# Differential attention's score maps: zero-padded query copies against half-height products issued in pairs

## The chip, the cores and the metric
The kernel runs on one core of a Trainium2 chip. It uses five engines with a queue each: TensorE (matrix products, PE in the profile, with its weight loads as PEld), VectorE (DVE), ScalarE (ACT), GpSimd (POOL) and SyncE (SP, which here issues the DMAs of weights). The metric is the device time of one execution in microseconds (us), the median over several runs.

## The reference
The program is the trunk of a diffusion generator: four layers over 256 latent and 256 context tokens of 1024 features, each a token mixer (another one in each layer) and an MLP. The change is in layer 1, differential attention with 8 heads. Cut to that:

```python
def _softmax_probs(q, k, scale):
    s = jnp.einsum("bhqd,bhkd->bhqk", q, k).astype(jnp.float32) * scale
    return jax.nn.softmax(s, axis=-1)

def project(t, positioned):                     # 128 features a head, two halves of 64
    q, k, v = (_heads(a, DIFF_HEADS) for a in jnp.split(t @ w_in, 3, axis=-1))
    if positioned: ...                          # rotates both halves of q and k (latent tokens)
    return q[..., :hd], q[..., hd:], k[..., :hd], k[..., hd:], v

def attend(q1, q2, k1, k2, v):
    p = _softmax_probs(q1, k1, scale) - lam * _softmax_probs(q2, k2, scale)
    o = jnp.einsum("bhqk,bhkd->bhqd", p.astype(v.dtype), v)
    return _rms_norm(o, subln) * (1.0 - lambda_init)
```

Each head has two attention maps, one from the first 64 features of its queries and keys and one from the last 64. Latent queries see the keys of all 512 tokens, context queries those of the 256 context tokens. The mixed map is multiplied with the values, and the result is normalised over the head's 128 features.

## The kernel before, in words
Activations lie with features on partitions and tokens along the columns: 256 latent columns (`S` of them), then 256 context columns (`T2` = 512 in all). Products with weights take operands split into a high and a low part (`mm3`, lines 294 to 296, three products each, the weight's parts made by lines 277 and 278 from 512 KB blocks that SP loads ahead). Everything else in layer 1 is multiplied in full float32, which TensorE runs as two instructions per product.

`mixer1` first makes the values of all heads (`proj_v`), and then runs a loop over 8 heads. Beside the attention of head h the generator `project(h + 1)` makes the next head's queries and keys: per head two blocks (`proj1`, 8 input tiles of three products of 512 columns each), each copied out of PSUM by ScalarE (lines 956 and 963) and rotated by `rope` (a product with a permutation at line 654, then VectorE, lines 655, 656 and 658). `aside(n)` takes its next n steps; in head 7 it takes steps of the output projection instead (`early`).

Queries are kept in `qz`, two sets (for even and odd heads) of two tiles of 128 partitions. Tile e holds the 64 features of map e on their own partitions and zeros on the other 64, written once by four memsets on POOL. So the score product of map e has all 128 partitions of the keys as its other operand, and the zeros take away the half that does not belong. In each head the loop visits the latent queries (two tiles of 128, keys of 512 columns) and then the context queries (two tiles, 256 columns). For one such query tile and each of the two maps:

- line 992: the scores, into a tile of the PSUM pool `sc`, which has two banks in turn;
- `softmax`: VectorE's maximum (line 664) and its factor (665), ScalarE's exponential (666) with the sum read back after it, VectorE's reciprocal (667).

Then VectorE mixes the maps (996 to 998), TensorE transposes the mixed map (1001), ScalarE copies it out of PSUM (1004), and up to three steps of the next head's projections follow in the program. After two query tiles the product with the values is made (1014) and copied (1016). After both streams `finish(h)` normalises the head: a square on ScalarE (971), a sum over partitions on TensorE (646, from `rsqrt_sum`), a scaled copy (647), a logarithm, an exponential and a square on ScalarE, and three VectorE instructions (529, 530, 973).

The order of instructions in each engine's queue is not the order of the program text. A scheduler lays it out when the program is built, going by text order as priority, by its own idea of durations and by when tiles and banks come free; on the chip each engine then takes its queue in that order. `DIFF_ROWS` gives the number of buffers of each ring of tiles: two for `k`, five for `p` (the maps), four for `pt`, four for `x`, two for `f`.

In layer 3, `gdn_chain` has products of 64 partitions: line 1594 takes the two halves of the partitions in turn, each into a bank of its own.

Of the kernel before, what the change touches and what calls it, by code (L numbers as in the profile page):

```python
# [12 lines left out]
F32 = mybir.dt.float32  # L13
# [15 lines left out]
DIFF_ROWS = dict(k=2, p=5, pt=4, x=4, f=2)  # L29
# [18 lines left out]
class Cols:  # L48
    """Column layout of the packed per-feature parameters."""
# [19 lines left out]
def _wa(w, kc=8):  # L69
    """[K, F] -> [F/128, K/(128 kc), 128, kc * 128]: blocks that hold one tile of outputs."""  # L70
    k, f = w.shape
    w = w.reshape(k // (128 * kc), kc, 128, f // 128, 128)
    return np.ascontiguousarray(w.transpose(3, 0, 2, 1, 4)).reshape(f // 128, k // (128 * kc), 128, kc * 128)


def _wb(w):
    """[K, F] -> [F/512, K/256, 128, 2 * 512]: blocks that hold 512 outputs of 256 inputs."""
    k, f = w.shape
    w = w.reshape(k // 256, 2, 128, f // 512, 512)
    return np.ascontiguousarray(w.transpose(3, 0, 2, 1, 4)).reshape(f // 512, k // 256, 128, 1024)  # L80


def _rope(dim):
    """cos and signed sin of the axial positions: [128 features (whole heads), 256 tokens] each."""
# [10 lines left out]
def _layout(x):  # L95
    """Host side: arrays as the kernel reads them (transposed, cut and joined; no arithmetic)."""
# [40 lines left out]
    # rows 0-63 see (forward, backward) in the two passes over a token tile, rows 64-127 the other way round  # L137
# [18 lines left out]
class Trunk:  # L156
    def __init__(self, ctx, tc, ins, out):
        self.ctx, self.tc, self.nc, self.I, self.out = ctx, tc, tc.nc, ins, out
        # what a layer norm is cut into
# [32 lines left out]
    def open_acc(self, pool):  # L192
        """Banks for products in turn from a pool of two and from that for projections beside other work."""
        acc, pj = ("acc", pool("acc", 2, space=PSUM)), ("pj", self.pj)
        turn = cycle((acc, acc, pj, pj))

        def tile():
            n, p = next(turn)
            return p.tile([128, T2], F32, name=n)
        self.acc = tile  # L200

    def proj1(self, block, n=T2, kc=8, x=None, every=2):
        """As proj, for one block and from the pool for projections beside other work; yields after every few input tiles."""
# [20 lines left out]
    def after(self, ins, other):  # L224
        """ins comes after other, of the same engine."""
# [9 lines left out]
    def tables(self):  # L235
        """Loads the tables of exp and ln, both, after the last silu."""
# [5 lines left out]
    def weights(self, *key):  # L242
        """One block of weights, split; the blocks that come after it are loaded and split ahead."""
# [13 lines left out]
    def load(self, name, *at):  # L257
        """Loads one block of weights and splits it: hi + lo, both with at most 12 significant bits; some stay whole."""
# [13 lines left out]
    def halved(self, pool, src, n=""):  # L272
        """Up to 1024 columns from DRAM, split."""
# [7 lines left out]
    def blocks(self):  # L281
        """The blocks of weights in the order of their use."""
# [15 lines left out]
    def proj(self, blocks, n=T2, t0=0, kc=8, x=None, outer=None, spare=False):  # L298
        """Yields PSUM tiles [128 features, n tokens]; blocks: weight blocks, one per output tile.
        outer: output widths of blocks whose products go together, input tile by input tile.  # L300
        spare: the first product goes to another pool."""
# [32 lines left out]
    def ada_prepare(self):  # L334
# [3 lines left out]
        # stationary operands of 32 columns: both conditions, and sums of partitions into one column or the other  # L338
# [8 lines left out]
        # picks the streams' rows from each quarter, or their sums over the quarters  # L347
# [4 lines left out]
    def begin(self, raw, blocks):  # L352
        """The first sub-layer's input, tile by tile as its modulation arrives, and beside it the products with the
        first blocks of weights, which arrive between; returns those products."""
# [57 lines left out]
    def aside(self, n=None):  # L412
        """The next n steps of the modulation that is worked out beside other things."""
        for _ in islice(self.beside, n):
            pass

    def ada(self, i):
        """Modulation of layer i: mods[:, 8 * kind + tile, stream]; yields 8 times for each kind (begin makes the first two of
        layer 0).  The products of layer 0 are TensorE's, those of the others, which come beside an MLP, VectorE's."""
# [37 lines left out]
    def coef(self, i, sub, r):  # L457
        """u = n * A + B and the gate for layer i, sub-layer sub, stream r; n is -2 times the normalised stream, without gain."""
# [28 lines left out]
    def ln_add(self, d, a, b):  # L487
        """Takes columns a to b of tile d of z, complete (the first two tiles come with all their columns).
        Sums are about c, the mean of the features of the first two tiles; it is taken from the others beforehand."""
# [19 lines left out]
    def ln_finish(self, a, b):  # L509
        """Mean (of what is left of z) and -2 / deviation of columns a to b."""  # L510
# [11 lines left out]
    def rsqrt(self, out, x):  # L522
        """out = -2 (x + eps) ** -0.5: the tables' value and one Newton step; x is overwritten."""
# [15 lines left out]
    def coefs(self, i, sub, t=T2):  # L539
        """All that turns the normalised parts into the input of a sub-layer, and its gates."""  # L540
# [3 lines left out]
    def enter(self, sub, r):  # L544
        """u (split) and the residual of a sub-layer from stream r, normalised."""
# [21 lines left out]
    def last_tiles(self, blocks, x, kc, sub):  # L567
        """The last four output tiles before a layer norm, part by part: what follows it begins with one
        part while the other is still under way.  sub: what follows, or None at the end."""
# [22 lines left out]
    def last_part(self, sub):  # L592
        """What is left of a layer norm, to be made once the next sub-layer has begun."""
# [6 lines left out]
    def mlp(self, i, t, following=None):  # L600
        """following: makes the coefs of the sub-layer after it, which is entered."""
# [40 lines left out]
    def rsqrt_sum(self, out, s, n, t):  # L642
        """out = -2 (sum over partitions of s / n + eps) ** -0.5, on all partitions; s is overwritten."""
# [6 lines left out]
    def rope(self, x, swapped, tab, out):  # L650
        """x: [128, >= 256] in SBUF; swapped: scratch; out: list of (destination, partitions)."""
# [8 lines left out]
    def softmax(self, p, ps, n, scale):  # L660
        """p = exp(scale * ps - max); returns 1 / sum per partition."""
# [19 lines left out]
    def early(self, name, n=7):  # L681
        """The products of the first n input tiles with the first two blocks of an output projection."""
# [31 lines left out]
    # the order of the projections of the gated linear attention, after the first four  # L714
# [16 lines left out]
    # the order of the other projections of the gated delta rule, after the first keys  # L731
# [15 lines left out]
    def mixer0(self, i):  # L747
        nc, I = self.nc, self.I
        with ExitStack() as ctx:
# [9 lines left out]
            def gather(raw, blocks):  # L759
                """Copies of products and the sum of their squares."""  # L760
# [47 lines left out]
    def mla_heads(self, pool, vp, tab, cq, ck, kr):  # L808
# [7 lines left out]
        def project(quad):  # L816
            """Values of 4 heads, queries and keys of 2 pairs."""
# [32 lines left out]
        for pair in range(8):  # L850
# [6 lines left out]
            for e, (q, k) in enumerate(qk):  # L857
                hp = slice(64 * e, 64 * e + 64)
                pts = []
                for qt in range(4):  # L860
# [14 lines left out]
                    # pt[j][:, kt % 2, query]  # L875
# [19 lines left out]
    def proj_v(self, blocks, dst):  # L895
        """dst[:, token tile, :512] = u^T W, tokens on partitions; blocks: 4 weight blocks of 256 inputs."""
# [18 lines left out]
    def mixer1(self, i):  # L915
        nc, I = self.nc, self.I
        lam0 = 0.8 - 0.6 * math.exp(-0.3 * i)
        with ExitStack() as ctx:
# [16 lines left out]
            qz = [[big.tile([128, T2], F32, name=f"qz{a}{b}") for b in range(2)] for a in range(2)]  # L935
            for a in range(2):
                nc.gpsimd.memset(qz[a][0][64:128, :], 0.0)
                nc.gpsimd.memset(qz[a][1][0:64, :], 0.0)
# [9 lines left out]
            self.sc = pool("sc", 2, space=PSUM)  # L948
# [4 lines left out]
            def project(h):  # L953
                qp = yield from self.proj1(("diff_qk", h, 0))
                x, w, q = row("x"), row("x"), qz[h % 2]
                nc.scalar.copy(x, qp)
                self.rope(x, w, tab, [(q[e][halves[e]], halves[e]) for e in range(2)])
                for e in range(2):
                    nc.vector.tensor_copy(q[e][halves[e], S:], x[halves[e], S:])
# [19 lines left out]
            for h in range(8):  # L979
# [3 lines left out]
                for lat in (True, False):  # L983
# [3 lines left out]
                    for qt in range(2):  # L987
                        qa = (0 if lat else S) + 128 * qt
                        es = []
                        for e in range(2):  # L990
                            sc = self.sc.tile([128, T2], F32, name="sc")
                            nc.tensor.matmul(sc[:, :n], lhsT=q[e][:, qa:qa + 128], rhs=k[:, k0:T2], start=True, stop=True)
                            p = row("p")
                            es.append((p, self.softmax(p, sc, n, scale)))
                        (p, r1), (p2, r2) = es
# [21 lines left out]
                finish(h)  # L1017
            self.split(self.uh[:, 7], self.ul[:, 7], o[:, 7])

# [1 line left out]
    def mixer2(self, i):  # L1021
        nc, I = self.nc, self.I
        with ExitStack() as ctx:
# [84 lines left out]
            def decays(h, e):  # L1108
                """Of one direction: exp of the running log decays, of their negatives and of those up to the chunk's end."""
# [19 lines left out]
                # over a chunk: columns of e1  # L1129
# [738 lines left out]
```

## Time and profile before

| | |
|---|---|
| runs | 2791.73, 2790.97, 2787.93 us |
| median | 2790.97 us |
| profiled execution | span 2789.6 us, first to last instruction; no other time of it is given |
| TensorE busy | 2691.3 us (96%), 15728 products |
| VectorE busy | 2025.3 us (73%) |
| ScalarE busy | 1255.1 us (45%) |
| POOL busy | 47.9 us |
| DMA | 353.26 MB, mean 127 GB/s |

The profile is one execution on the chip. A group row reads: line, engine, operation, output<-inputs, shapes as partitions x columns (for TensorE rows*columns of the array that are used, then the moving operand), count, then busy time in us and mean ns of one, then idle time ahead of them and what ended it. Ends of products are modelled, and products overlap in the pipeline, so the distance from start to start tells more than a duration. A row of a timeline is its start in us, its length, engine, line, operation, names and count, where consecutive instructions of one kind are merged. A row of stretches has the stretch, its length, and for each engine its busy time with the number of instructions in brackets (PE, PEld, DVE, ACT, POOL), then the granted TensorE clock as a share of full speed (2.4 GHz), the DMA share and GB/s.

### The profile page before, as it was taken

What the parts mean: (1) busy time and instruction counts of PE and PEld (TensorE: products, weight loads), DVE (VectorE), ACT (ScalarE), POOL (GpSimd) and SP (SyncE); (2) the same over time, 40 slices, a digit from 0 to 9 for tenths busy, and PEclk for the clock granted to TensorE, in tenths of its full rate; (3) what the DMA queues carried; (4) which work ended last, traced back from release to release, by engine and by line L of the source; (5) the groups of instructions that cost most, each with busy time, mean ns of one, the idle gap of its engine ahead of it and who ended that gap; (6) DMA issues with size and microseconds to landing.
All of it is one profiled execution on the core that took longest, in us unless ns stands there. A gap on an engine that the chain in (4) does not pass through costs nothing. (4 is left out here: it accounts for less than half of the span.)

```text
span 2789.6 us, 41018 instructions
## 1 busy us (share of the span) xinstructions
PE 2691.3 (96%) x15728; PEld 2166.6 (78%) x15728; DVE 2025.3 (73%) x3908; ACT 1255.1 (45%) x2413; POOL 47.9 (2%) x75
## 2 busy tenths in 40 slices
PE   7999999999999989999999999999999998998998
PEld 5666787788876687888888887887887876657997
DVE  3666798784757799875754489876689897668666
ACT  3544453333545663332454455322354555444544
POOL 0000000000000000000000000000000111000000
PEclk9999999999999999999999999999999898999999
DMA  6533237564121126654311125664322445313453
GB/s 232 174 97 104 78 106 218 180 191 134 59 69 50 34 79 218 197 175 147 93 63 56 58 76 178 199 189 159 117 82 81 158 153 151 107 29 121 159 182 113
DMA packets 125536, 353.26 MB, mean 127 GB/s; under 512 B 37499, under 2 KB 41339, under 8 KB 124828
## 3 DMA queue, kind: packets, MB, share of 16 engines
q1 hardware_dynamic: 121804, 337.00, 38.3%
q0 software_dynamic: 3536, 13.63, 1.3%
q8 instruction: 124, 2.03, 0.3%
q14 instruction: 72, 0.59, 0.1%
HBM read 335.91 MB, written 14.68 MB: 126 GB/s over the span
## 5 line engine op out<-in xcount | busy, mean ns | idle before, releaser
L277 ACT CAST whi<-raw 128x1024 fp32r<-128x1024 f32 (+2 forms) x403 | 410.4, 1023 | 694.0 <-PE acc L295 259.9
L278 DVE TENSOR_TENSOR wlo<-raw,whi 128x1024 fp32r<-128x1024 f32 (+2 forms) x403 | 478.0, 1189 | 199.7 <-ACT whi L277 193.9
L294 PE MATMUL pj<-ul,whi 128*128 128x512 f32 (+1 forms) x1072 | 398.6, 372 | 1.1 <-DVE z L565 1.0
L296 PE MATMUL pj<-uh,wlo 128*128 128x512 f32 (+1 forms) x1072 | 386.9, 361 | 0.6 <-DVE wlo L278 0.6
L295 PE MATMUL pj<-uh,whi 128*128 128x512 f32 (+1 forms) x1072 | 386.2, 360 | 0.0
L438 DVE SCALAR_TENSOR_TENSOR acc<-raw,s,acc 128x1024 f32<-128x1024 f32 x252 | 317.2, 1280 | 31.8 <-DMA raw<-in_ada 28.7
L294 PE MATMUL acc<-ul,whi 128*128 128x512 f32 (+3 forms) x888 | 311.7, 351 | 15.9 <-DVE ul L554 11.0
L295 PE MATMUL acc<-uh,whi 128*128 128x512 f32 (+3 forms) x888 | 308.7, 348 | 0.0
L296 PE MATMUL acc<-uh,wlo 128*128 128x512 f32 (+3 forms) x888 | 308.5, 347 | 0.0
L294 PEld LDWEIGHTS pj<-ul,whi 128*128 128x128 f32 x1072 | 203.0, 189 | 37.4 <-issue 6.3
L296 PEld LDWEIGHTS pj<-uh,wlo 128*128 128x128 f32 x1072 | 203.0, 189 | 32.6 <-issue 4.6
L295 PEld LDWEIGHTS pj<-uh,whi 128*128 128x128 f32 x1072 | 203.2, 190 | 30.1 <-issue 5.8
L294 PE MATMUL pj<-hl,whi 128*128 128x512 f32 (+1 forms) x560 | 198.3, 354 | 0.7 <-DVE hl L621 0.3
L294 PEld LDWEIGHTS acc<-ul,whi 128*128 128x128 f32 (+2 forms) x888 | 167.2, 188 | 40.6 <-DVE ul L554 12.9
L295 PE MATMUL acc<-hh,whi 128*128 128x512 f32 (+1 forms) x560 | 197.5, 353 | 0.0
L294 PE MATMUL acc<-hl,whi 128*128 128x512 f32 (+1 forms) x560 | 196.8, 351 | 0.0
L295 PE MATMUL pj<-hh,whi 128*128 128x512 f32 (+1 forms) x560 | 196.7, 351 | 0.0
L296 PE MATMUL acc<-hh,wlo 128*128 128x512 f32 (+1 forms) x560 | 196.5, 351 | 0.0
L296 PE MATMUL pj<-hh,wlo 128*128 128x512 f32 (+1 forms) x560 | 196.2, 350 | 0.0
L296 PEld LDWEIGHTS acc<-uh,wlo 128*128 128x128 f32 (+2 forms) x888 | 167.1, 188 | 22.1 <-issue 1.2
L295 PEld LDWEIGHTS acc<-uh,whi 128*128 128x128 f32 (+2 forms) x888 | 167.3, 188 | 20.8 <-issue 1.0
L620 ACT CAST hh<-t 128x512 fp32r<-128x512 f32 (+1 forms) x128 | 72.2, 567 | 123.6 <-DVE t L619 123.2
(463 smaller groups left out, 5001.0 us busy)
## 6 DMA issues: line engine op xcount, KB each, us to landing
raw<-in_w SPq DMA_DIRECT2D x256, 512.0 KB, 4.2
raw<-in_ada SPq DMA_DIRECT2D x192, 512.0 KB, 4.7
raw<-in_diff_qk SPq DMA_DIRECT2D x16, 512.0 KB, 3.5
raw<-in_gdn_v SPq DMA_DIRECT2D x16, 512.0 KB, 4.0
raw<-in_gdn_z SPq DMA_DIRECT2D x16, 512.0 KB, 4.5
raw<-in_gdn_out SPq DMA_DIRECT2D x16, 512.0 KB, 3.9
raw<-in_mla_in SPq DMA_DIRECT2D x9, 512.0 KB, 7.5
raw<-in_mla_qb SPq DMA_DIRECT2D x12, 384.0 KB, 3.6
```

Source lines behind the costliest of these rows:

```text
L277: nc.scalar.copy(hi[:, :width], raw[:, :width])
L278: nc.vector.tensor_sub(lo[:, :width], raw[:, :width], hi[:, :width].bitcast(F32))
L294: mm(ps, lhsT=ah, rhs=bl, start=start, stop=False)
L295: mm(ps, lhsT=ah, rhs=bh, start=False, stop=False)
L296: mm(ps, lhsT=al, rhs=bh, start=False, stop=stop)
L438: nc.vector.scalar_tensor_tensor(acc[r], w, self.s[:, k, r:r + 1], acc[r], op0=ALU.mult, op1=ALU.add)
L620: nc.scalar.copy(hh[:, f, :t], r[:, :t])
```

## The change
The four `qz` tiles and their memsets go. The rotated query of a head is one tile of all 128 partitions, from the ring `k`, which has four buffers now, shared by queries and keys. The score product of map e takes partitions 0 to 63 or 64 to 127 of both queries and keys. The score pool has one buffer of two banks in place of two of one bank; both products of a query tile are issued one after the other in the text, each into a bank of this tile, and both softmaxes follow. `finish(h - 1)` stands behind the first score products of head h, not at the end of head h - 1; the last head's stands behind the loop. All else in the diff is comments and docstrings that become empty lines.

```diff
-DIFF_ROWS = dict(k=2, p=5, pt=4, x=4, f=2)
+DIFF_ROWS = dict(k=4, p=5, pt=4, x=4, f=2)
...
-            qz = [[big.tile([128, T2], F32, name=f"qz{a}{b}") for b in range(2)] for a in range(2)]
-            for a in range(2):
-                nc.gpsimd.memset(qz[a][0][64:128, :], 0.0)
-                nc.gpsimd.memset(qz[a][1][0:64, :], 0.0)
...
-            self.sc = pool("sc", 2, space=PSUM)
+            self.sc = pool("sc", 1, space=PSUM)
...
-                x, w, q = row("x"), row("x"), qz[h % 2]
+                x, w, q = row("x"), row("x"), row("k")
                 nc.scalar.copy(x, qp)
-                self.rope(x, w, tab, [(q[e][halves[e]], halves[e]) for e in range(2)])
-                for e in range(2):
-                    nc.vector.tensor_copy(q[e][halves[e], S:], x[halves[e], S:])
+                self.rope(x, w, tab, [(q, slice(0, 128))])
+                nc.vector.tensor_copy(q[:, S:], x[:, S:])
...
-                        es = []
-                        for e in range(2):
-                            sc = self.sc.tile([128, T2], F32, name="sc")
-                            nc.tensor.matmul(sc[:, :n], lhsT=q[e][:, qa:qa + 128], rhs=k[:, k0:T2], start=True, stop=True)
-                            p = row("p")
-                            es.append((p, self.softmax(p, sc, n, scale)))
-                        (p, r1), (p2, r2) = es
+
+                        both = self.sc.tile([128, 2, T2], F32, name="sc")
+                        scs = [both[:, e] for e in range(2)]
+                        for sc, hp in zip(scs, halves):
+                            nc.tensor.matmul(sc[:, :n], lhsT=q[hp, qa:qa + 128], rhs=k[hp, k0:T2], start=True, stop=True)
+                        if h and lat and qt == 0:
+                            finish(h - 1)
+                        (p, r1), (p2, r2) = [(p, self.softmax(p, sc, n, scale)) for sc in scs for p in [row("p")]]
...
-                finish(h)
+            finish(7)
             self.split(self.uh[:, 7], self.ul[:, 7], o[:, 7])
```

## Rows read from the trace of the kernel before

**Rows 1.** Stretches: head 3, head 7, and the sum over all eight heads.
```profile
862.90:885.40 22.50, 22.46 (x95) 15.79 (x94) 17.01 (x51) 13.22 (x33) 0.00 (x0) 1.00 0.15 47
...
954.80:975.00 20.20, 18.82 (x74) 11.93 (x74) 12.26 (x40) 12.25 (x33) 0.00 (x0) 1.00 0.00 1
sum 180.20, PE 177.86 PEld 124.10 DVE 135.50 ACT 105.19 POOL 0.00; mean PE 22.23 PEld 15.51 DVE 16.94 ACT 13.15 POOL 0.00
```

**Rows 2.** Groups by line and shape, 794 to 976 us.
```profile
L992 PE MATMUL sc<-k,qz 128*128 128x512 f32 x64 | 33.0, 602 | 0.0
...
L992 PEld LDWEIGHTS sc<-k,qz 128*128 128x128 f32 x128 | 22.4, 189 | 11.3 <-issue 4.3 <-ACT p L666 3.1 <-DVE k L658 0.2
L666 ACT ACTIVATE p<-sc,sm 128x512 f32<-128x512 f32 x32 | 22.1, 691 | 6.7 <-DVE sm L665 6.6
L664 DVE TENSOR_REDUCE sm<-sc 128x1 f32<-128x512 f32 x32 | 22.1, 689 | 18.8 <-PE sc L992 18.8
L992 PE MATMUL sc<-k,qz 128*128 128x256 f32 x64 | 17.9, 382 | 0.0
...
L666 ACT ACTIVATE p<-sc,sm 128x256 f32<-128x256 f32 x32 | 15.3, 478 | 12.2 <-DVE sm L665 11.3 <-DVE sm L667 0.4
...
L666 ACT ACTIVATION_READ_ACCUMULATOR p<-sc,sm 128x1 f32 x64 | 12.9, 201 | 0.0
L664 DVE TENSOR_REDUCE sm<-sc 128x1 f32<-128x256 f32 x32 | 12.8, 418 | 10.4 <-PE sc L992 10.1
...
L665 DVE TENSOR_SCALAR sm<-sm 128x1 f32<-128x1 f32 x64 | 9.3, 147 | 0.4
...
L658 DVE TENSOR_TENSOR qz<-x 64x256 f32<-64x256 f32 x14 | 5.8, 415 | 0.1
```

**Rows 3.** Waits, 795 to 975 us: us in total, times, longest.
```profile
PEld ax L1001 <- DVE p L998: 7.7, 15, 1.6
...
PEld st L646 <- ACT f L971: 4.8, 8, 0.6
...
PEld sc L992 <- ACT p L666: 3.1, 11, 0.6
```

**Rows 4.** Timeline of TensorE, first latent query tiles of head 1.
```profile
820.10 1.02 PE L992 MATMUL sc<-k,qz 128*128 128x512 f32 x2
...
821.19 0.40 PE L295 MATMUL pj<-uh,whi 128*128 128x512 f32 x1
821.42 0.40 PE L296 MATMUL pj<-uh,wlo 128*128 128x512 f32 x1
821.66 1.08 PE L992 MATMUL sc<-k,qz 128*128 128x512 f32 x2
...
822.81 0.39 PE L295 MATMUL pj<-uh,whi 128*128 128x512 f32 x1
```

**Rows 5.** Timeline of TensorE, second context query tile of head 1.
```profile
834.25 1.03 PE L992 MATMUL sc<-k,qz 128*128 128x256 f32 x4
...
835.34 0.39 PE L295 MATMUL pj<-uh,whi 128*128 128x512 f32 x1
```

**Rows 6.** Timeline of TensorE: half-height products in layer 3, full-height ones in layer 1.
```profile
2392.56 1.13 PE L1594 MATMUL st<-t,kt 64*128 64x256 f32 x8
2393.62 0.60 PE L1607 MATMUL ax<-t,at 128*128 128x128 f32 x3
...
967.60 1.89 PE L1014 MATMUL st<-pt,v 128*128 128x256 f32 x8
969.33 0.38 PE L1001 MATMUL ax<-ident,p 128*128 128x128 f32 x2
```

**Rows 7.** Timeline of TensorE in head 7: latent scores, and the last sum of squares.
```profile
954.86 1.02 PE L992 MATMUL sc<-k,qz 128*128 128x512 f32 x2
...
958.19 1.10 PE L992 MATMUL sc<-k,qz 128*128 128x512 f32 x2
...
973.51 1.12 PE L646 MATMUL st<-f,ones 128*128 128x512 f32 x2
```

## The prediction
> **What bounds the kernel now.** I read the stretches by head first. In a head of the middle of layer 1's loop, 22.5 us long, TensorE is busy 22.46 us at full granted clock, VectorE 17.0 (76%), ScalarE 13.2; over all eight heads TensorE has 177.9 of 180.2 us [rows 1]. So TensorE sets the end of heads 0 to 6. Only the last head is open: 1.4 us of its stretch are without TensorE [rows 1].
>
> Then the groups by line, for the scores of line 992: 64 instructions of 512 columns and 64 of 256 [rows 2]. The shape `128*128` is the point: all rows of the array are used, and half of them multiply the zeros of `qz`. One product in full float32 is two instructions, so there are 32 maps of each width.
>
> Then the waits. TensorE's weight loads wait 7.7 us for the mixed map ahead of the transposes, 4.8 for the square ahead of the sum of squares, 3.1 for an exponential that frees a score bank [rows 3]: little beside 180 us.
>
> **The scores.** Durations of TensorE's rows overlap, so I take distances between starts. One latent map: from 820.10 to the second weight product at 821.19 is 1.09 us for two score instructions and one weight product; weight products follow each other at 0.23 (821.19 to 821.42), so the map holds TensorE 0.86 us. The next map, alone among weight products, runs from 821.66 to 822.81: 1.15 - 0.23 = 0.92, or 0.06 for its own change of operand kind [rows 4]. A latent query tile costs 0.86 + 0.92 = 1.78. Two context maps stand together: 834.25 to 835.34 less one weight product is 0.86 [rows 5].
>
> Do two maps on the two halves of the partitions run at once? Layer 3 has the same form: line 1594 multiplies 64 rows at a time, from either half in turn, into two banks. Eight such instructions of 256 columns take 1.06 us until the next line starts; eight of full height (line 1014) take 1.73 [rows 6], 0.216 each. Four in succession would be 0.86, so the halves overlap fully and 0.20 goes into beginning and end. That group began after a wait; for leaving a running stream of weight products I add the 0.06 of rows 4. A joint pair then costs 0.86 + 0.26 = 1.12 for a latent tile and 0.43 + 0.26 = 0.69 for a context tile: 0.66 and 0.17 saved. Heads 0 to 6 have 14 of each: 14 x 0.83 = 11.6 us. Bounds: with nothing lost at the borders 14 x (0.92 + 0.43) = 18.9; with no overlap and the border still paid, a loss of 14 x (0.20 + 0.26) = 6.4. I stay by line 1594, the nearest row.
>
> Rows 6 hold a group that entered an empty array. On that the Trainium skill ("TensorEngine Tiling (Array Packing)", Tiling Modes) speaks against the change: tiles run in parallel, but a change of the tiling mode drains the engine. If nothing of a pair could be loaded before that drain, a weight load of 189 ns [rows 2] would show at each of 28 pairs, 5.3 us, and the sum below would be -3.6 in place of -8.9. No row shows a switch by rows out of weight products.
>
> **The single score tile.** Both banks are now one buffer. The next pair waits until the second exponential has read; before, each map waited for its own bank's. That is later by one exponential and its sum, 0.69 + 0.20 [rows 2]. Behind the waiting pair TensorE has everything in its queue: weight products, transposes, values. The cover is that a head has 48 weight products (11 us), which the order, fixed when the program is built, lays between. Now 3.1 us in 11 places are lost in this way [rows 3]; I add half of that, 1.5 (0, if the products between suffice, to 28 x 0.89 = 25).
>
> **The transposes.** They need the mixed map, for which VectorE takes the maximum of the first map, then of the second (689 ns each, a 147 ns factor behind each). That the second map is there 0.86 us sooner helps nothing while VectorE works on the first. So TensorE comes up to 0.66 sooner to a transpose whose input comes no sooner. If all 15 waits of now [rows 3] grew so, about half of them latent, it would be 8 x 0.66 + 7 x 0.17 = 6.5 us; if weight products fill it, 0. I take a third, 2.0.
>
> **finish moved.** The norm of head h - 1 (a sum on TensorE, five ScalarE and three VectorE instructions) comes after the next head's first scores are issued. The 0.6 us per head in which the load for the sum waits for the square [rows 3] lies partly beside a running score instruction (0.43); the rest, 0.2, goes seven times: -1.3. What is late next is that head's first exponential, queued on ScalarE behind the square, as it is now.
>
> **Edits at nothing.** The rotation writes one tile, not two halves: 14 additions of 415 ns [rows 2] become 7, and the copies of line 959 halve too; 2.9 us of VectorE and more, hidden while TensorE bounds, and a help where (d) below comes about. The four memsets on POOL lie ahead of the loop, beside the value projections; uncovered they would be a gain. No DMA is added or moved, and SP's queue stays as it is.
>
> **Head 7.** It is nearer to a chain: 18.65 us from its first score at 954.86 to the last sum at 973.51 [rows 7], with 42 weight products as filler, and the single tile forbids scores ahead. From the first latent tile to the second there are 3.33 us (954.86 to 958.19); the new cycle is a pair 1.12, two maxima and factors 1.68, an exponential and its sum 0.89, or 3.7. I set +0.5 (-3 if TensorE still bounds, as in the other heads, to +4 with 1 us lost per tile).
>
> **Sum.** -11.6 + 1.5 + 2.0 - 1.3 + 0.5 = -8.9 us against the profiled span of 2789.6, so 2780.7. The median of the runs shown is 1.4 above that span: 2782.
>
> **The rivals.**
> (a) All of it comes through: enough weight products lie between, no wait is added, head 7 gains its share: 16 x 0.83 + 1.3 = 14.6, so 2776. For it: 48 products of 0.23 against four cycles that need 1.7 to 2.6 us of cover each. Against it: an order that was fixed ahead. Chance 0.18.
> (b) The order swallows it: where TensorE gets ahead it waits for VectorE, 6.5 instead of 2.0, and 3.1 instead of 1.5 for the tile: -2.8, so 2788. The waits of rows 3 are many and short, as where an input is awaited just in time. Chance 0.18.
> (c) The maps don't overlap here, something standing between them in the queue. Only borders are left, 0 to +6.4: 2794. Line 1594 speaks against it. Chance 0.07.
> (d) Slower: the single tile makes VectorE and ScalarE one chain. A latent cycle is 3.7, a context one 0.69 + 2 x 0.42 + 2 x 0.15 + 0.48 + 0.20 = 2.5, together 12.4 per head; VectorE's other work is 17.0 - 0.4 - 5.6 (its part of the cycles) = 11.0. If none of that fits into the gaps of the cycles a head takes 23.4, and with some 0.2 for each of four hand-overs to VectorE 24.2, against 22.5. It decides from where VectorE hides less than 1.7 us per head; at half a microsecond hidden it is +1.2 per head, +8 in all: 2799. Against it: each pair is itself such a gap, 3.6 us per head. Chance 0.11.
>
> **How the numbers follow.** My forecast has 0.46, by itself 2779 to 2786. The range, 2774 to 2796, takes in (a), (b) and most of (c) and leaves out (d). A measurement of this kernel tells about 0.2% (5.6 us) from no change. Faster by more (under 2785.4): of mine 0.40, of (a) 0.17, of (b) 0.03, so 0.60. Slower by more (over 2796.6): 0.09 of (d) and 0.02 of (c), so 0.11. The rest, 0.29, is the same.
>
> **What would show it.** In the trace after: score instructions in 64 rows, the four of a tile holding TensorE 1.0 to 1.2 us (latent) and 0.6 to 0.75 (context); heads of 21.3 to 21.7 us in place of 22.5; the scores' wait for exponentials at 4 to 5 us, the transposes' for the mixed map near 10, the sum's for the square near 0; VectorE near 80% of a head. It is wrong if the four starts of a latent tile lie 0.43 apart in single file (c), if heads grow with TensorE idle ahead of scores (d), or if the loop shrinks and a later layer gives it back.

## The result, and the profile after

The changed kernel is slower: 2831.44 us against 2791.35 for the kernel before in the same comparison, a ratio of 1.0148 (95% interval 1.0134 to 1.0161), four runs each. 2782 was predicted, with a range to 2796. The profiled spans are 2827.9 and 2789.6.

Nearly all of it arises in layer 1's loop. From the first score product to the second instruction of the last sum of squares there were 179.2 us (794.89 to 974.05) and are now 215.8 (796.67 to 1012.48), so 36.6 of the 38.3 us. What lies behind the loop takes 1815.5 us in both traces. The other 1.8 us lie ahead of the loop, which starts between 790.5 and 796.7 us in the fourteen profiles of this case; they tell nothing.

Stretches of the changed kernel (columns as in [rows 1]): heads 2 to 7, each from its first score to the next head's, the last to its sum of squares. Heads 0 and 1 have 24.73 and 25.42 us at full clock.
```profile
846.82:872.72 25.90, 22.48 (x94) 15.24 (x93) 17.16 (x49) 13.56 (x34) 0.00 (x0) 0.93 0.13 40
872.72:897.64 24.92, 21.40 (x96) 14.21 (x95) 17.15 (x49) 13.46 (x34) 0.00 (x0) 1.00 0.15 43
897.64:923.67 26.03, 22.83 (x95) 15.27 (x95) 17.16 (x49) 13.48 (x34) 0.00 (x0) 0.93 0.12 41
923.67:952.96 29.29, 26.16 (x104) 17.89 (x103) 21.00 (x55) 17.42 (x41) 0.00 (x0) 0.88 0.11 36
952.96:978.18 25.22, 20.10 (x79) 12.74 (x78) 15.25 (x47) 11.19 (x31) 0.00 (x0) 0.86 0.06 21
978.18:1012.48 34.30, 25.63 (x62) 14.46 (x62) 13.14 (x40) 12.41 (x32) 0.00 (x0) 0.65 0.00 1
```
Head 3 stands against the first row of [rows 1]: 24.92 us for 22.50, with TensorE busy 21.40 for 22.46. So 3.5 us of that head are now without TensorE, where there was next to nothing (0.04), and VectorE and ScalarE have what they had (17.15 and 13.46 us). No engine got more work in this head; they wait for one another. The column behind POOL is the granted clock: it was 1.00 throughout the loop before, and falls below that in heads 2, 4, 5, 6 and 7.

Waits of the changed kernel, 796 to 1014 us (us in total, times, longest):
```profile
ACT p L666 <- DVE sm L665: 48.1, 39, 4.5
DVE sm L667 <- ACT p L666: 35.0, 43, 1.5
...
PEld sc L988 <- ACT p L666: 26.6, 19, 4.8
...
PEld ax L997 <- DVE p L994: 10.7, 14, 1.9
...
PEld st L646 <- ACT f L966: 4.5, 6, 0.8
```
The third row answers to the scores' wait of [rows 3]: 26.6 us, and up to 4.8 at a time, where 3.1 and at most 0.6 were lost. The two rows above it go together: ScalarE's exponential waits for VectorE's factor (48.1 us; 17.9 before), and VectorE's reciprocal for ScalarE's exponential (35.0; 1.5 before). Before, over 795 to 975 us:
```profile
ACT p L666 <- DVE sm L665: 17.9, 18, 4.3
...
DVE sm L667 <- ACT p L666: 1.5, 4, 0.5
```
That is what a chain between two engines looks like: each of them waits for the other, neither is full.

One latent query tile of the changed kernel, head 2 (timeline of all engines, some rows; the brackets have idle time and what ended it):
```profile
853.26 1.13 PE L988 MATMUL sc<-k 64*128 64x512 f32 x4
...
855.47 0.68 DVE L664 TENSOR_REDUCE sm<-sc 128x1 f32<-128x512 f32 x1
...
856.92 0.69 ACT L666 ACTIVATE p<-sc,sm 128x512 f32<-128x512 f32 x1 [1.23 <-DVE sm L665]
...
857.73 0.16 DVE L667 RECIPROCAL sm<-sm 128x1 f32<-128x1 f32 x1 [0.85 <-ACT p L666]
857.81 0.67 DVE L664 TENSOR_REDUCE sm<-sc 128x1 f32<-128x512 f32 x1
...
858.79 0.15 DVE L665 TENSOR_SCALAR sm<-sm 128x1 f32<-128x1 f32 x1
...
858.97 0.69 ACT L666 ACTIVATE p<-sc,sm 128x512 f32<-128x512 f32 x1 [0.34 <-DVE sm L665]
...
859.80 0.70 PE L988 MATMUL sc<-k 64*128 64x256 f32 x4 [2.73 <-ACT p L666]
```
Both maps' scores are there at 854.39. The second map's maximum begins at 857.81, 3.4 us later, right behind the first map's exponential, and the next tile's scores only behind the second map's. The two maps' softmaxes do not overlap at all: from pair to pair 2.21 us to the first maximum (the scores, and VectorE's work on what went before), 1.45 to the first exponential, 0.81 for it, 1.24 for reciprocal, second maximum and factor, 0.83 for the second exponential. That is 6.54 us for one of four tiles of a head.

Granted clock in head 7 of the changed kernel (stretches of 4 us):
```profile
976.00:980.00 4.00, 3.98 (x16) 2.11 (x16) 1.82 (x4) 1.37 (x3) 0.00 (x0) 1.00 0.00 0
980.00:984.00 4.00, 0.37 (x1) 0.00 (x0) 1.78 (x7) 3.53 (x7) 0.00 (x0) 1.00 0.00 0
984.00:988.00 4.00, 3.42 (x7) 1.55 (x8) 3.19 (x7) 1.11 (x4) 0.00 (x0) 0.51 0.02 4
988.00:992.00 4.00, 4.00 (x8) 1.98 (x7) 1.29 (x4) 1.20 (x4) 0.00 (x0) 0.50 0.01 2
```
The score product that this stretch of idling ends with:
```profile
984.32 2.07 PE L988 MATMUL sc<-k 64*128 64x512 f32 x2 [3.95 <-ACT p L666]
```
TensorE does nearly nothing for 4 us, because its next score product waits 3.95 us for an exponential; then it has work again, but at 0.50 of the clock, the lower level of 1.2 GHz. There the two score instructions of a map that stands alone take 2.07 us; at full clock they take 1.12 (848.33, in the kernel with half height alone below).

### The profile page after: what moved, and what is told of

The parts are those of the page before. It is cut to its first block, busy times and chain, and to the rows that moved or that the text cites. A ratio compares the mean times of both kernels' runs of the same rounds, so it can differ in the third digit from the quotient of the medians.

```text
span 2827.9 us, 41019 instructions
## 1 busy us (share of the span) xinstructions
PE 2701.5 (96%) x15728; PEld 2167.5 (77%) x15728; DVE 2023.5 (72%) x3892; ACT 1257.1 (44%) x2413; POOL 46.2 (2%) x71
## 5 line engine op out<-in xcount | busy, mean ns | idle before, releaser
L294 PE MATMUL pj<-ul,whi 128*128 128x512 f32 (+1 forms) x1072 | 391.9, 366 | 0.7 <-DVE sm L665 0.5
```

Source lines behind the costliest of these rows:

```text
L294: mm(ps, lhsT=ah, rhs=bl, start=start, stop=False)
```

## The experiments

Theory A: the one tile of two banks is the cause. It has three variants. A1: VectorE's second maximum waits for ScalarE's first exponential because both read the same tile. A2: the next pair waits until both maps have been read. A3: the reciprocal stands ahead of the second maximum in VectorE's queue. The rivals: B, the moved `finish`; C, the half-height products and the changes between them and full height. None of the kernels leaves out part of the computation.

**Two tiles of one bank** (after, changed):
```diff
-            self.sc = pool("sc", 1, space=PSUM)
+            self.sc = pool("sc", 2, space=PSUM)
-                        both = self.sc.tile([128, 2, T2], F32, name="sc")
-                        scs = [both[:, e] for e in range(2)]
+                        scs = [self.sc.tile([128, T2], F32, name="sc") for e in range(2)]
```


> The changed kernel, but with two one-bank score tiles (a pool of two) in place of one two-bank tile; the half-height products are still issued one behind the other, finish still moved. Theory A (readers of one PSUM tile are kept in text order across engines, so VectorE's maximum of map 1 waits for ScalarE's exponential of map 0, and the four query tiles of a head become chains of 6.3 us): the wait is gone, heads fall from 25.5 to 21.5-22.5 us, no stretch of the loop at half clock, 2778 to 2790 us. Theory B (finish at its new place holds up the first softmax): still 2815 to 2831. Theory C (half-height products leave TensorE so little activity that its clock is halved): half-clock stretches stay in the loop, 2810 to 2831.


Measured: 2793.83 against 2787.96, ratio 1.0021 (1.0009 to 1.0032). The same two banks, taken one by one, give back most of the loss (5.9 us above before, where the change has 40.1): the loop has 183.2 us, at full clock throughout. The time is still 4 us above the range that theory A gave; the expected gain is missing, and the second latent tile of a head shows a reason, in seven of the eight heads.
```profile
842.98 1.12 PE L987 MATMUL sc<-k 64*128 64x512 f32 x2 [0.48 <-ACT p L666]
...
844.70 1.12 PE L987 MATMUL sc<-k 64*128 64x512 f32 x2
```
Its two maps stand apart (x2 each, 1.72 us from one to the other, weight products between), and the first waits for its bank. A map that is alone saves nothing by its half height (the kernel with half height alone, below, has its price).

**The text of the softmaxes interleaved, still one tile** (after, changed):
```diff
-  (p, r1), (p2, r2) = [(p, self.softmax(p, sc, n, scale)) for sc in scs for p in [row("p")]]
...
+  for m, sc in zip(ms, scs):
+      nc.vector.reduce_max(m[:, 0:1], sc[:, :n], axis=AX.X)
+      nc.vector.tensor_scalar_mul(m[:, 1:2], m[:, 0:1], -scale)
+  for m, sc, x in zip(ms, scs, (p, p2)):
+      nc.scalar.activation(x[:, :n], sc[:, :n], AF.Exp, scale=scale, bias=m[:, 1:2], accum_out=m[:, 2:3])
+  for m in ms:
+      nc.vector.reciprocal(m[:, 3:4], m[:, 2:3])
...
```


> The changed kernel with its single two-bank tile, but the text takes both maxima, both factors, both exponentials, both reciprocals in this order. Theory A (order of readers): VectorE's second maximum no longer waits; what is left of the single tile is that the next pair waits for both exponentials, a cycle of 1.12 + 1.68 + 0.69 + 0.89 = 4.4 us for a latent tile in place of 6.4; heads 22 to 23 us, 2783 to 2800. Rival A2 (the joint release of both banks is what costs, not the order of readers): heads stay above 24.5 us, 2815 to 2831.


Measured: 2802.83 against 2787.96, 1.0055 (1.0034 to 1.0075), loop 193.9 us. With the same tile, banks and release, text order alone takes off nearly two thirds of the loss (0.93 of 1.48 points), though the time lies 3 us above the range of theory A. Of the 0.55 that are left, the kernel with two tiles still has 0.21; the rest is the joint release, A2, and that the first exponential now waits for the second maximum, which no run separates. Waits of this kernel, 794 to 990 us:
```profile
PEld sc L988 <- ACT p L997: 13.0, 14, 3.0
...
ACT p L997 <- DVE sm L994: 10.3, 4, 2.8
```
The last row is that wait, in four places: line 994 is the maximum, line 997 the exponential.

**`finish` back at the head's end** (after, changed):
```diff
-                        if h and lat and qt == 0:
-                            finish(h - 1)
...
-            finish(7)
+                finish(h)
```


> The changed kernel with finish(h) back at the end of each head. Theory A: the chain of readers is untouched, 2824 to 2838. Theory B (the moved finish is the cause): 2778 to 2795.


Measured: 2835.82, 1.0169 (1.0142 to 1.0196), loop 226.8 us. B falls: put back, it is no faster. The intervals of this and of the change overlap a little, so that the move helps is likely, not shown.

**Half height alone** (after, with two one-bank tiles, each map's product and softmax in the text order of before, `finish` at the head's end):
```diff
...
+  for e in range(2):
+      sc = self.sc.tile([128, T2], F32, name="sc")
+      nc.tensor.matmul(sc[:, :n], lhsT=q[halves[e], qa:qa + 128], rhs=k[halves[e], k0:T2], start=True, stop=True)
+      p = row("p")
+      es.append((p, self.softmax(p, sc, n, scale)))
...
```


> The kernel before, with one query tile and half-height score products, but its own order: scores and softmax of map 0, then of map 1, in two one-bank tiles, finish at the end of a head. Theory A: no chain; where the two maps are apart in TensorE's queue they don't overlap, where they stand together they do: 2783 to 2793, clock full in the loop. Theory C (half-height products lower the clock): stretches at half clock in the loop, 2800 to 2830.


Measured: 2805.61, 1.0061 (1.0038 to 1.0084). Slower than theory A allowed, and inside the range of C. Three heads of this kernel as a stretch, and one latent map of it:
```profile
844.27:918.56 74.29, 73.50 (x284) 44.54 (x283) 50.60 (x147) 41.38 (x100) 0.00 (x0) 1.00 0.14 43
```
```profile
848.01 0.39 PE L296 MATMUL pj<-uh,wlo 128*128 128x512 f32 x1
848.33 1.12 PE L988 MATMUL sc<-k 64*128 64x512 f32 x2
849.38 0.50 PE L294 MATMUL pj<-ul,whi 128*128 128x512 f32 x1
849.71 0.40 PE L295 MATMUL pj<-uh,whi 128*128 128x512 f32 x1
```
Here TensorE is full (73.50 of 74.29) at full clock, which it has over the whole loop, and yet a head has 24.76 us. So half height does not bring the clock down, as C had it, but it has a price of its own: from the product before to the second one behind there are 1.70 us, less two products of 0.23 is 1.24 for a lone map. By the same reckoning the full-height map of [rows 4] has 0.93 (821.42 to 822.81, 1.39 less 0.46). Such a head has four lone latent maps at 1.24 and two lone context maps at 0.82 (853.03 to 854.31 in this kernel, less 0.46); against 1.78 and 0.86 for a tile before that makes 2.2 us more, an estimate, and the head is longer by 2.1.

**The single tile alone** (the kernel before, changed; queries stay full height with zeros):
```diff
-            self.sc = pool("sc", 2, space=PSUM)
+            self.sc = pool("sc", 1, space=PSUM)
...
+                        both = self.sc.tile([128, 2, T2], F32, name="sc")
+                        scs = [both[:, e] for e in range(2)]
```
with both products first and both softmaxes behind. That order by itself is in the kernel with two tiles and, at full height, in a twin with four banks further down (+0.08%) too, and costs nothing like this.


> The kernel before with one edit: the single two-bank score tile, both score products issued one behind the other and both softmaxes after them. Queries stay in the zeroed copies, products at full height, finish at the end of a head. Theory A (the shared tile chains VectorE and ScalarE): the harm comes without any half-height product; heads of 25 to 28 us, half clock in the last heads, 2825 to 2850 us. Theory C (half-height products are the cause): 2786 to 2796.


Measured: 2848.51 against 2788.15, 1.0216 (1.0199 to 1.0233), loop 238.1 us. This part alone costs more than the whole change. Waits, 796 to 1035 us:
```profile
ACT p L666 <- DVE sm L665: 41.5, 37, 2.9
...
DVE sm L667 <- ACT p L666: 36.6, 49, 1.4
PEld sc L992 <- ACT p L666: 34.5, 23, 5.0
```
The same three rows as in the changed kernel, without any half-height product. A holds, and what else the change does helps beside it: 2.16% less 1.48% is 0.7%. Some of that lies in the queries, their lower products and smaller rotation: the changed kernel with `finish` put back, which differs from this one in them and their buffers alone, has 1.69% (1.0142 to 1.0196).

**Reciprocals last, still one tile** (after, changed: per map maximum, factor and exponential):
```diff
-  (p, r1), (p2, r2) = [(p, self.softmax(p, sc, n, scale)) for sc in scs for p in [row("p")]]
+  for m, sc, x in zip(ms, scs, (p, p2)):
+      nc.vector.reduce_max(...); nc.vector.tensor_scalar_mul(...); nc.scalar.activation(...)
+  for m in ms:
+      nc.vector.reciprocal(m[:, 3:4], m[:, 2:3])
```


> The changed kernel with its single tile; the text is changed so that both reciprocals stand after both exponentials. Theory A1 (the tile: the second maximum is given a wait for the first exponential because both read one tile): the wait moves from the reciprocal to the second maximum and nothing is won, 2822 to 2840 us. Rival A3 (the reciprocal of map 0 stands in VectorE's queue ahead of the second maximum and blocks it): the second maximum goes ahead, heads near 23.5 as where all maxima came first, 2795 to 2810.


Measured: 2821.16, 1.0114 (1.0099 to 1.0129), loop 211.6 us. A3 is at most the smaller part: the reciprocal has gone from ahead of the second maximum, which is worth 0.34 points, far from the range of A3; for the rest the wait has only moved to the maximum itself (line 994 now; 794 to 1008 us):
```profile
DVE sm L994 <- ACT p L996: 22.9, 23, 1.5
PEld sc L988 <- ACT p L996: 19.8, 18, 4.1
```
The built instruction streams say it outright. VectorE's, for one tile, with what each instruction waits for (instructions of other work between them left out):
```
changed kernel                            reciprocals last                      two tiles
L664 TENSOR_REDUCE sm<-sc  [PE]           L994 TENSOR_REDUCE sm<-sc [PE]          L664 TENSOR_REDUCE sm<-sc [PE]
L665 TENSOR_SCALAR         [DVE]          L995 TENSOR_SCALAR        [DVE]         L665 TENSOR_SCALAR        [DVE]
L667 RECIPROCAL            [Activation]   ...                                     L664 TENSOR_REDUCE sm<-sc [PE]
L664 TENSOR_REDUCE sm<-sc  (no wait)      L994 TENSOR_REDUCE sm<-sc [Activation]  L665 TENSOR_SCALAR        [DVE]
```
With one tile the second maximum waits for ScalarE, in the middle stream by itself, on the left through the reciprocal just ahead of it; with two tiles it waits for TensorE alone. It is so in all 32 query tiles of the loop. In these kernels two engines that only read one PSUM tile, each map in a bank of its own, are thus kept in the order of the text. A1 is shown by this, by the two tiles and by the interleaved text (1.14% to 0.55% with the reciprocals last in both); why the build orders two readers I did not find out.

**Four banks: the second query tile of each stream takes its banks from `st`** (two tiles, changed):
```diff
-  scs = [self.sc.tile([128, T2], F32, name="sc") for e in range(2)]
+  pool_, name_ = (self.st, "st") if qt else (self.sc, "sc")
+  scs = [pool_.tile([128, T2], F32, name=name_) for e in range(2)]
```


> The changed kernel with four one-bank score tiles: the first query tile of a pair of tiles takes two from the score pool, the second takes two from the pool of the value products and sums. All products are still issued in pairs, no two maps share a tile, and a pair need not wait for the one before. Theory A with borders as the trace of the kernel after has them (a pair costs 1.25 us latent, 0.82 context, against 1.78 and 0.86): 16 x (0.53 + 0.04) = 9 us less in the loop, some 1 us from finish: 2776 to 2784 where before is 2790; no half clock in the loop. If what is left of the slowness is half-height products as such: 2792 to 2800.

Its twin has the same banks and order, with the zeroed queries of before at full height (shown against the half-height one; it keeps `qz` and its memsets):
```diff
-  nc.tensor.matmul(sc[:, :n], lhsT=q[hp, qa:qa + 128], rhs=k[hp, k0:T2], start=True, stop=True)
+  nc.tensor.matmul(sc[:, :n], lhsT=q[e][:, qa:qa + 128], rhs=k[:, k0:T2], start=True, stop=True)
```


> As the kernel with four score banks, but with zeroed query copies and products of full height (as before): issued together, and unable to overlap. If the overlap is what gains: 2787 to 2793, some 8 us above the half-height one. If the gain is from the banks or the moved finish: equal to it.

Measured: 2791.92, 1.0013 (1.0003 to 1.0024); the twin 2791.39, 1.0008 (0.9999 to 1.0017). No gain, and no difference between the two heights (heads of 22.74 and 22.76 us on average). The second latent pair was split again, since its second bank is held by `finish`'s sum: its weight load waits for the scaled copy of that sum (line 647), 1.0 us in each of four heads. So I moved `finish`, each time with the full-height twin.

**Four banks, `finish` behind the second latent pair:**
```diff
-                        if h and lat and qt == 0:
+                        if h and lat and qt == 1:
```


> As the kernel with four score banks, but finish(h - 1) stands behind the scores of the second latent tile, so that its sum no longer holds one of the two banks which that tile needs: both latent pairs of a head stand one behind the other in TensorE's queue, all 64 rows high. Theory A with borders: both pairs should take about 2.1 us and what follows, against 3.6 at full height, and a head 21.2 to 21.8 us where before has 22.7: 2778 to 2784 where before is 2790. Rival (TensorE no longer bounds a head, VectorE's and ScalarE's chain does, and overlap is won in vain): the products overlap, heads stay at 22.5 or more, 2788 to 2794.

> The same order and banks with zeroed query copies and products of full height. If the overlap of halves is what gains: 2788 to 2794, 6 to 12 us above the half-height one. If both are equal, TensorE does not bound a head here.

Measured: 2791.19, 1.0009 (0.9999 to 1.0020), and the twin 2791.45, 1.0008 (0.9998 to 1.0019). TensorE in the half-height one:
```profile
863.86 0.40 PE L296 MATMUL pj<-uh,wlo 128*128 128x512 f32 x1
864.19 1.13 PE L988 MATMUL sc<-k 64*128 64x512 f32 x4
865.15 1.02 PE L988 MATMUL st<-k 64*128 64x512 f32 x4
...
866.45 0.39 PE L295 MATMUL pj<-uh,whi 128*128 128x512 f32 x1
...
869.21 1.13 PE L646 MATMUL st<-f,ones 128*128 128x512 f32 x2 [1.44 <-ACT p L666]
```
Now two latent tiles pass in 2.13 us (863.86 to 866.45, less two products of 0.23), where the prediction counted 2 x 1.78 = 3.56 before. The 1.43 so saved are lost at 869.21, where TensorE waits 1.44: the sum needs a bank, and the exponential that frees it comes no sooner. The twin shows it:
```profile
862.20 0.40 PE L296 MATMUL pj<-uh,wlo 128*128 128x512 f32 x1
862.43 1.88 PE L992 MATMUL sc<-k,qz 128*128 128x512 f32 x4
...
866.10 0.39 PE L295 MATMUL pj<-uh,whi 128*128 128x512 f32 x1
...
867.35 1.12 PE L646 MATMUL st<-f,ones 128*128 128x512 f32 x2
```
Its two latent tiles take 3.44 us (862.20 to 866.10, less 0.46), its sum does not wait, and it starts 4.92 us behind the first score, where the half-height kernel has 5.02.

**Four banks, `finish` behind the first context pair:**
```diff
-                        if h and lat and qt == 1:
+                        if h and not lat and qt == 0:
```


> Four score banks, half-height pairs, finish(h - 1) behind the first context scores of head h: its sum takes its bank after both latent pairs have been read, so the wait of 1.6 us that the sum had behind the second latent pair should be gone, and no weight product stands between the two latent pairs. If it was that wait that used up the overlap: heads of 21.3 to 22.0 us, 2778 to 2785 where before is 2788 to 2790. If the order is bound by VectorE and ScalarE all the same: another wait takes its place, heads 22.5 or more, 2786 to 2794.

> The same banks and place of finish with zeroed query copies at full height. If the overlap pays in the kernel with half-height products: this one 5 to 10 us above it. If TensorE does not bound a head in this order: equal within 3 us.

Measured: 2789.94, 1.0004 (0.9995 to 1.0013), and the twin 2790.10, 1.0000 (0.9990 to 1.0011). TensorE in the half-height one, behind both latent pairs:
```profile
866.98 0.50 PE L294 MATMUL pj<-ul,whi 128*128 128x512 f32 x1
868.34 0.63 PE L997 MATMUL ax<-ident,p 128*128 128x128 f32 x4 [0.86 <-DVE p L994]
```
The sum's wait is gone here, and the transposes wait instead: 1.36 us from the weight product to them, 0.86 of it idle. The same 90 us of both, the half-height kernel and its twin:
```profile
840.00:930.00 90.00, 86.66 (x382) 59.59 (x383) 64.86 (x197) 55.80 (x136) 0.00 (x0) 1.00 0.15 48
```
```profile
840.00:930.00 90.00, 89.83 (x380) 65.28 (x379) 68.56 (x205) 54.49 (x134) 0.00 (x0) 1.00 0.15 47
```
Half height takes 3.2 us off TensorE's busy time here, in about as many products, and the loop is no shorter: 180.2 us against the twin's 178.9. Heads 1 to 6 have 135.6 and 135.5 us; in head 7 the half-height kernel has 4 us at a granted clock of 0.62 (956 to 960) that the twin has not, and is longer there by 1.6. No kernel that I ran is faster than the one before, and the three with half height and four banks, which I expected to gain, gained nothing.

## Why the prediction was wrong

**The single score tile** is the step that failed: I set +1.5, with a bound of 25 for the joint release. I counted only that the next pair is released later by one exponential. What the step did not see is that the two softmaxes of one tile no longer overlap. The runs with the tile alone (+60.4 us) and without it (+5.9, where the change has +40.1) show that it carries most of the loss, and the interleaved text that the larger part of this is the order of the readers (0.93 points, of which 0.34 go with the place of the reciprocals), not the release.

**Rival (d)** was the right direction and was given 0.11. It had the chain, but with both maxima in a row, ahead of the exponentials, and so a cycle of 3.7 us latent; the tile above took 6.54, and the expected 2799 was too low by 32. It also left out what idle time does to the clock. By the same cut the heads before had 23.4, 22.9, 22.5, 22.8, 22.5, 22.9, 23.0 and 19.2 us. Heads 0, 1 and 3, still at full clock, are longer by 1.3, 2.6 and 2.1, 2.0 on average; eight times that is 16 of the 36.6 us, an estimate of the chain alone. The other 20.6 lie in the five heads with a lowered clock (longer by 3.4, 3.5, 6.4, 2.3 and 15.1, less 2.0 each); for head 7, the last of them, I had +0.5. (The 42 weight products that I counted as filler there are those of the text; in the trace before, 26 lie between head 7's first score and last sum, in the trace after 18.) How they divide between the clock and a longer chain, with less to lay between in head 7, no run separates: that is open.

**The scores.** The maps do overlap, so rival (c) is wrong: the four instructions of a pair start together by twos (single starts in the trace: 796.671 and 796.678, then 797.205 and 797.211), 0.53 us apart. But the borders were too cheap. TensorE in the changed kernel, first tile of head 0:
```profile
796.35 0.40 PE L295 MATMUL pj<-uh,whi 128*128 128x512 f32 x1
796.67 1.13 PE L988 MATMUL sc<-k 64*128 64x512 f32 x4
797.73 0.50 PE L296 MATMUL pj<-uh,wlo 128*128 128x512 f32 x1
798.07 0.40 PE L294 MATMUL pj<-ul,whi 128*128 128x512 f32 x1
```
796.35 to 798.07 is 1.72, less two products of 0.23 is 1.26, where I had 1.12. The border is 0.40, not the 0.26 from [rows 6] and [rows 4]. From the pair's first start to the next line's there are 1.06 us, which is 0.20 over its columns as for line 1594. But the weight product ahead of it holds 0.32 (796.35 to 796.67) and the one behind it 0.34 (797.73 to 798.07) instead of 0.23: another 0.20, where I had 0.06. [Rows 6] could not show it, as that group had nothing ahead of it and I stopped at the next start. The border is the same for a context tile:
```profile
839.13 0.40 PE L294 MATMUL pj<-ul,whi 128*128 128x512 f32 x1
839.46 0.70 PE L988 MATMUL sc<-k 64*128 64x256 f32 x4
...
840.42 0.40 PE L296 MATMUL pj<-uh,wlo 128*128 128x512 f32 x1
```
1.29 less 0.46 is 0.83. A latent tile saves 0.52 instead of 0.66, a context tile 0.03 instead of 0.17, and 14 of each 7.7 us instead of 11.6. 28 borders of 0.14 more are 3.9 us, against the 5.3 that I worked out for a switch and set aside. On this step the Trainium skill ("TensorEngine Tiling (Array Packing)", Tiling Modes) was the better guide: a change of tiling mode drains the engine. The trace agrees in so far as each change costs something, 0.40 us a pair; that it is a drain no run shows.

**The transposes, and rival (b).** Without the chain, (b) is what remains: the kernels with four banks save TensorE's time and lose it again to a bank or to the mixed map, to within 0.1% of their full-height twins. So the +2.0 of new waits should have been nearly all of the gain. [Rows 1] misled me: that TensorE is busy 22.46 of 22.50 us does not say that the softmaxes would be ready if it came sooner. The short waits of [rows 3] did say so.

**`finish`.** The sign may be right, the reason isn't: the load for the sum still waits 4.5 us for the square (4.8 in [rows 3]). The term was also summed loosely: seven times 0.2 is 1.4, seven times 0.6 - 0.43 is 1.2.

**Edits at nothing** stood, as far as is known: POOL's memsets and the rotation's half-height instructions are gone (VectorE is busy 134.0 us in the loop instead of 135.5), but no run takes them apart.

Of the marks that the prediction named, it was the one of (d) that came: heads grow with TensorE idle ahead of scores, and the scores' wait for exponentials, foretold at 4 to 5 us, was 26.6. The transposes' wait, 10.7 us, is near the 10 foretold; VectorE's share of a head went to 69% in head 3, not to 80, as the head grew and its work didn't.

## What to carry to other kernels

Before two tiles become one, list all that read them, by engine and in text order: a reader on a second engine can turn two parallel chains into one, though no data passes between them. A busy share of 100% doesn't say that a cut in that engine's work pays; look how late the next engines deliver what it needs behind the cut. And where a change can leave TensorE idle for some microseconds, count the granted clock of what follows.

## What the runs showed of the hardware

- Two half-height float32 products on the two halves of the partitions run side by side, but at full clock a pair of 512 columns costs 0.40 us beyond the 0.86 of its columns where it stands among full-height products, and a lone map pays about the same (1.24 us, for 0.93 at full height).
- In the changed kernel, behind 4 us in which TensorE was busy for 0.37 us (980 to 984), the granted clock was 0.51, and it was 0.50 in the stretch of 988 to 992 us, in which TensorE was busy throughout. Before the change no stretch of 4 us of the loop was below full clock, nor in the kernels with half height alone and with two score tiles; each of the kernels with the single score tile had some that were.
